# Six pools and their pads: where the tiles of a two-block float32 kernel begin in SBUF

## The chip, the cores and the metric

The kernel runs on one core of one Trainium2 chip. The metric is the device time of one launch in microseconds (us), the median of several runs. The profile is of one execution on the same core.

## What is computed

The reference is two transformer blocks on a sequence of 256 tokens of width 1024, each block two layers deep, all in float32:

```python
def first_block(x, c, ...):                       # 2 layers
    mod = silu(c) @ w_ada[l] + b_ada[l]
    h = rms_norm(x, g_norm1[l]) * (1 + sc1) + sh1
    u = h @ w_in[l] + b_in[l]
    y_mla = causal_softmax_attention(q, k, v_mla)
    y_sb = stick_breaking_attention(q_sb, k_sb, v_sb)
    merged = sigmoid(gate_mla) * (y_mla @ w_branch_mla[l]) + sigmoid(gate_sb) * (y_sb @ w_branch_sb[l])
    x = x + gt1 * (merged @ w_out[l])
    up = causal_depthwise_conv(h2 @ w_up[l], w_conv[l], b_conv[l])
    x = x + gt2 * ((silu(a) * v_ff) @ w_down[l])  # d_ff 2816

def second_block(x, c, ctx, ...):                 # 2 layers, latent and context tokens
    p = modulate(rmsnorm(x), sh1, sc1) @ w_in[l]
    x = x + gt1 * latent_mixer(p, ctx_kv, ...)    # global and window attention, short conv, gates
    x = x + gt2 * expert_choice_ffn(h2, ...)      # 16 experts, 32 tokens each, hidden 1024
```

The weights are read from HBM once; the page counts 739 MB.

## The kernel before

Activations stand feature-major: a tile `[128, 8, 256]` holds 1024 features in eight slices of 128 partitions and 256 tokens, so a slice is 1024 bytes of each partition. Tiles are taken by tag in `Kernel.t` (line 154): each tag has a fixed number of slots in the pool `sb`, and the tags lie one after another in the order in which they are first used.

Most products are made of float32r parts. A weight block comes by DMA into a `w` tile; `split` (line 216) has ScalarE cast it into `wh` and VectorE subtract the cast into `wl`. The activations are split likewise: `hh` and `hl` hold the normalized input of a layer, `pt` the merged branches of the second block, `k1` and `k8` the outputs of heads, branches and the feed-forward. `mm3` (line 229) then issues three matmuls for each slice of 128 features:

```python
for k in range(len(w)):
    (wh, wl), (xh, xl) = w[k], x[k]
    ops += [(wh, xh), (wh, xl), (wl, xh)]
for i, (a, b) in enumerate(ops):
    self.last_mm = self.nc.tensor.matmul(ps, a, b, ...)   # line 235
```

The first operand is the stationary one: 128 columns, 512 bytes of each partition, loaded by a LDWEIGHTS of its own. The second is the moving one: 256 columns, 1024 bytes. So in the order of TensorE's queue the moving operand goes `hh`, `hl`, `hh` slice by slice while the stationary ones go `wh`, `wh`, `wl`. In `first_layer`, `ffn` (`lower`, line 828, with the products of the feed-forward in two `k1` tiles), `mixer` and `out_proj` all large products run so. `tokens` (line 716) and part of `kv` have it the other way round, with `hh` or `hl` stationary and `wh` or `wl` moving. The products of the experts (`product`, line 1239, and line 1291) are plain float32 with 32 stationary columns, and their moving operands are the weights as they come by DMA, in `w`, `k8`, `k4`, `hh`, `hl`, `wh` and `wl` slots. Plain float32 matmuls are two instructions each on TensorE.

Where the tags lie follows from the widths of the tiles ahead of them. In the program before, `k1` and `k8` begin 384 bytes past a multiple of 1024, `w` 960, and `hh`, `hl`, `k2`, `wh`, `wl`, `k4` and `pt` all 320. Slices of a stationary operand are 512 bytes apart and slices of a moving one 1024. So the moving operand begins 0 or 512 bytes (mod 1024) from the stationary one where it is `hh`, `hl` or `pt`, and 64 or 576 where it is `k1` or `k8`. In the rows of a profile buffer numbers are left out: `k` stands for `k1`, `k2`, `k4` and `k8` together.

Of the kernel before, what the change touches and what calls it, by code (L numbers as in the profile page):

```python
# [9 lines left out]
F32 = mybir.dt.float32  # L10
# [7 lines left out]
P = 128  # L18
# [20 lines left out]
NH = 3  # L39
HALVES = {"k4": ("k4", "k4"), "whl": ("wh", "wl")}  # L40
BUFS = {"k4": N4, "wh": NH, "wl": 3}

CONST_WIDTHS = [
    [("ident", P), ("slot", 1), ("freq", 1), ("eps", 1), ("halfpi", 1), ("one", 1), ("sign", 1), ("ones", P), ("mask_m", P)],
# [53 lines left out]
class Stats:  # L98
    def __init__(self, kernel, x, bank=None, proj=None):
        self.kernel, self.x, self.ps, self.bank, self.proj = kernel, x, None, bank or kernel.ad, proj  # L100
# [22 lines left out]
class Kernel:  # L123
    def __init__(self, tc, ctx, io, out, consts):
        self.tc, self.nc, self.io, self.out = tc, tc.nc, io, out
        self.n = 0
        self.one = ctx.enter_context(tc.tile_pool(name="one", bufs=1))
        self.sb = ctx.enter_context(tc.tile_pool(name="sb", bufs=1))
        self.ps = ctx.enter_context(tc.tile_pool(name="ps", bufs=1, space=PSUM))
        self.cst = self.one.tile([P, NCONST], F32, name="cst")  # L130
        self.nc.sync.dma_start(self.cst[:, :NFIRST], consts[:, :NFIRST])
        self.consts = consts
        self.rt = self.one.tile([P, 2, S], F32, name="rope")
        self.fill = []
        self.wsel = 0
        self.table, self.head, self.users, self.before = None, None, [], []
        self.hook, self.last_mm = None, None
        self.ada_tags, self.ada_tag = [], "w"
# [14 lines left out]

    def t(self, shape, tag, bufs, dt=F32):
        self.n += 1
        return self.sb.tile(list(shape), dt, name=f"{tag}_{self.n}", tag=tag, bufs=bufs)

    def k8(self, shape, dt=F32):
        return self.t(shape, "k8", N8, dt)
# [43 lines left out]
    def wload(self, src, k0, nk, c0, nc_, tag="w"):  # L203
        t = self.wtile([P, nk, nc_], tag)
        self.nc.sync.dma_start(t, src[k0 * P:(k0 + nk) * P, c0:c0 + nc_].rearrange("(k p) n -> p k n", p=P))
        return t
# [19 lines left out]
    def wsplit1(self, src, shape):  # L226
        return self.wsplit(shape, [(src, lambda t: t)])
# [73 lines left out]
    def to_fm(self, src_dram, dst):  # L301
        nc = self.nc
        tm = self.k8([P, 2, D])
        nc.sync.dma_start(tm, src_dram.rearrange("(t p) d -> p t d", p=P))
        for t in range(2):
            for g in range(2):
                ps = self.mm((P, 4, P))
                for i in range(4):
                    k = 4 * g + i
                    nc.tensor.transpose(ps[:, i], tm[:, t, k * P:(k + 1) * P], self.c("ident"))  # L310
                nc.vector.tensor_copy(dst[:, 4 * g:4 * g + 4, t * P:(t + 1) * P], ps)
# [874 lines left out]
    def expert_loads(self, l, early, ring):  # L1186
# [13 lines left out]
        def more(n):  # L1200
            late = []
            for _ in range(min(n, len(todo))):
# [3 lines left out]
                if tag in HALVES:  # L1206
                    parts = [self.t([P, nk // 2, width], i, BUFS[i]) for i in HALVES[tag]]
                else:
# [267 lines left out]
```

## Time and profile before

| | |
|---|---|
| median of 3 runs | 2857.3 us (2854.14 to 2861.59) |
| profiled execution | 2864.09 us, of which the span is 2862.3 us |
| PE busy | 2663.3 us (93%) in 18816 matmul instructions |
| of these on line 235 | 10572 |
| DVE, ACT, POOL busy | 1406.6, 1022.9, 122.8 us |
| DMA | 742.61 MB, mean 259 GB/s, up to 409 GB/s in slices of 71.6 us |
| mean granted TensorE clock | 0.972 |

PE rows give matmuls; their ends are modelled and overlap, so the time that one takes in a stream is read from the distance of two starts, or from a stretch divided by its number of matmuls, and not from the duration in the row. PEld rows give the loads of stationary operands, which overlap the matmul ahead of them. A MATMUL row is named after its output, its moving and its stationary operand (`dd<-hh,wh`).

### The profile page before, as it was taken

What the parts mean: (1) busy time and instruction counts of PE and PEld (TensorE: products, weight loads), DVE (VectorE), ACT (ScalarE), POOL (GpSimd) and SP (SyncE); (2) the same over time, 40 slices, a digit from 0 to 9 for tenths busy, and PEclk for the clock granted to TensorE, in tenths of its full rate; (3) what the DMA queues carried; (4) which work ended last, traced back from release to release, by engine and by line L of the source; (5) the groups of instructions that cost most, each with busy time, mean ns of one, the idle gap of its engine ahead of it and who ended that gap; (6) DMA issues with size and microseconds to landing.
All of it is one profiled execution on the core that took longest, in us unless ns stands there. A gap on an engine that the chain in (4) does not pass through costs nothing.

```text
span 2862.3 us, 45431 instructions
## 1 busy us (share of the span) xinstructions
PE 2663.3 (93%) x18816; PEld 1847.5 (65%) x18816; DVE 1406.6 (49%) x2791; ACT 1022.9 (36%) x1906; POOL 122.8 (4%) x139
## 2 busy tenths in 40 slices
PE   7998999999999999899999999999899998877776
PEld 4898998888998689756994333333566994212122
DVE  5989977756777755776552011010577552000001
ACT  3564555554555644445453000001455442000000
POOL 0100001000000000120011000000021001000000
PEclk7999999999999999979999999999999999999998
DMA  8697855687555579412755999999712866999999
GB/s 291 226 325 273 319 175 164 199 267 230 171 178 192 162 247 268 140 39 82 199 162 219 367 401 401 409 402 389 248 62 71 262 213 261 409 409 408 409 409 318
DMA packets 397692, 742.61 MB, mean 259 GB/s; under 512 B 16214, under 2 KB 270126, under 8 KB 397486
## 3 DMA queue, kind: packets, MB, share of 16 engines
q1 hardware_dynamic: 396398, 738.66, 72.6%
q8 instruction: 148, 2.42, 0.3%
q10 hardware_dynamic: 1088, 1.05, 0.1%
q14 instruction: 58, 0.48, 0.0%
HBM read 738.61 MB, written 1.05 MB: 258 GB/s over the span
## 4 chain that ended last, share of the span: by engine, by line
PE 39%; DMA 13%; DVE 2%; POOL 1%; ACT 1%; SPq 0%; issue 0%; DVEq 0%; POOLq 0%; ACTq 0%
PE dd L235 12%; PE acc L1239 12%; PE mm L1239 5%; DMA w<-in_w_e_down_dram 3%; DMA w<-in_w_e_up_dram 2%; DMA k<-in_w_e_down_dram 2%; PE acc L931 2%; DMA k<-in_w_e_gate_dram 2%; DMA k<-in_w_e_up_dram 2%; DMA w<-in_w_e_gate_dram 2%; PE mm L960 1%; PE mm L954 1%; PE acc L1291 1%; PE dd L1272 1%; POOL k L746 1%; PE mm L1169 1%
## 5 line engine op out<-in xcount | busy, mean ns | idle before, releaser
L235 PE MATMUL dd<-hh,wh 128*128 128x256 f32 x2384 | 692.2, 292 | 17.6 <-ACT hh L259 13.9
L218 DVE TENSOR_TENSOR wl<-w,wh 128x1024 fp32r<-128x1024 f32 (+1 forms) x534 | 555.3, 1043 | 284.8 <-ACT wh L217 283.3
L235 PE MATMUL dd<-hh,wl 128*128 128x256 f32 x2384 | 684.8, 288 | 5.6 <-DVE wl L218 5.6
L235 PE MATMUL dd<-hl,wh 128*128 128x256 f32 x2384 | 684.0, 287 | 0.5 <-DVE hl L471 0.3
L217 ACT CAST wh<-w 128x1024 fp32r<-128x1024 f32 (+1 forms) x534 | 477.2, 899 | 563.5 <-PE dd L235 426.7
L235 PEld LDWEIGHTS dd<-hh,wh 128*128 128x128 f32 x2384 | 460.9, 194 | 43.6 <-ACT hh L259 15.6
L235 PEld LDWEIGHTS dd<-hh,wl 128*128 128x128 f32 x2384 | 461.3, 194 | 12.4 <-DVE wl L218 6.7
L235 PEld LDWEIGHTS dd<-hl,wh 128*128 128x128 f32 x2384 | 462.0, 194 | 10.0 <-issue 7.2
L1239 PE MATMUL acc<-w,pt 128*32 128x512 f32 x624 | 226.1, 605 | 34.5 <-DMA w<-in_w_e_up_dram 18.1
L1261 DVE TENSOR_TENSOR wh<-wh,acc 128x512 f32<-128x512 f32 x20 | 13.8, 688 | 460.3 <-PE acc L1239 460.3
L1239 PE MATMUL acc<-k,pt 128*32 128x512 f32 x692 | 227.7, 602 | 9.7 <-DMA k<-in_w_e_up_dram 5.8
L235 PE MATMUL dd<-k,wh 128*128 128x256 f32 x896 | 164.6, 283 | 1.8 <-DVE k L619 1.0
L746 POOL TENSOR_TENSOR k<-k,rope 32x256 f32<-32x256 f32 (+1 forms) x96 | 86.5, 901 | 1838.6 <-DVE k L890 1339.1
L1239 PE MATMUL acc<-w,k 128*32 128x512 f32 x480 | 160.6, 607 | 0.6 <-ACT pt L1139 0.6
L1239 PE MATMUL acc<-w,wl 128*32 128x512 f32 x396 | 140.1, 602 | 17.1 <-DMA w<-in_w_e_down_dram 17.1
L1239 PE MATMUL acc<-k,wl 128*32 128x512 f32 x432 | 147.0, 600 | 6.0 <-DMA k<-in_w_e_down_dram 6.0
L235 PEld LDWEIGHTS dd<-k,wh 128*128 128x128 f32 x896 | 137.5, 188 | 5.9 <-DVE k L619 1.6
L1239 PEld LDWEIGHTS acc<-w,pt 128*32 128x32 f32 x624 | 46.4, 110 | 138.3 <-issue 72.5
L1239 PE MATMUL acc<-k,k 128*32 128x512 f32 x376 | 133.2, 604 | 0.0
L235 PE MATMUL dd<-k,wl 128*128 128x256 f32 x448 | 125.2, 280 | 1.7 <-DVE wl L218 1.6
L1273 DVE SCALAR_TENSOR_TENSOR x_res<-dd,mod,x_res 128x256 f32<-128x256 f32 x64 | 28.9, 483 | 178.1 <-PE dd L1272 178.1
L1239 PEld LDWEIGHTS acc<-k,pt 128*32 128x32 f32 x692 | 46.0, 109 | 99.7 <-issue 65.3
(351 smaller groups left out, 4475.1 us busy)
## 6 DMA issues: line engine op xcount, KB each, us to landing
w<-in_w_in_dram SPq DMA_DIRECT2D x104, 1024.0 KB
w<-in_w_ada_dram SPq DMA_DIRECT2D x63, 1024.0 KB
w<-in_w_e_gate_dram SPq DMA_DIRECT2D x54, 1024.0 KB
w<-in_w_e_up_dram SPq DMA_DIRECT2D x54, 1024.0 KB
w<-in_w_e_down_dram SPq DMA_DIRECT2D x48, 1024.0 KB
w<-in_w_up_dram SPq DMA_DIRECT2D x44, 1024.0 KB
k<-in_w_e_gate_dram SPq DMA_DIRECT2D x43, 1024.0 KB
k<-in_w_e_down_dram SPq DMA_DIRECT2D x43, 1024.0 KB
```

The lines of the kernel that those rows point to most:

```text
L217: self.nc.scalar.copy(h, src)
L218: self.nc.vector.tensor_tensor(l, src, h.bitcast(F32), op=OP.subtract)
L235: self.last_mm = self.nc.tensor.matmul(ps, a, b, start=first and i == 0, stop=last and i == len(ops) - 1, skip_group_check=group)
L746: nc.gpsimd.tensor_tensor(u[dst], q[src], sin[src], op=OP.mult)
L931: nc.tensor.matmul(ps[:, :n], q[a, mt, qb * P:(qb + 1) * P], kk[a, br, lo:512], start=True, stop=not mask, skip_group_check=True)
L954: nc.tensor.transpose(pp[:, i], e[:, i * P:(i + 1) * P], self.c("ident"))
L960: nc.tensor.matmul(po[64 * f:64 * f + 64], vv[:, kt, P * br + 64 * f:P * br + 64 * f + 64], pt[:, f, i], start=i == 0, stop=i == len(kts) ...
L1169: nc.tensor.matmul(ps, th[:, t, a], b, start=t == 0, stop=False)
L1239: nc.tensor.matmul(accs[s][n][32 * e:32 * e + 32], lhs(s, 2 * kp + k, e), tiles[e][k][:, 512 * n:512 * n + 512], start=kp == 0 and k == 0, ...
L1272: nc.tensor.matmul(ps, y[:, k * P:(k + 1) * P], maps[s][:, gi], start=True, stop=True)
L1273: nc.vector.scalar_tensor_tensor(x[:, k], ps, gate[:, k:k + 1], x[:, k], op0=OP.mult, op1=OP.add)
L1291: nc.tensor.matmul(ps[32 * e:32 * e + 32], down(s, k, e), tiles[e][k], start=k == 0, stop=k == KT - 1, skip_group_check=True)
```

## The change

Twelve of the tags leave the pool `sb` for six pools of their own, which lie ahead of it in this order; some pools begin with a gap tile that no instruction touches. `PADS` counts float32 columns, so the gaps are 64, 32, 32, 128 and 32 bytes. The pool `one` gets a tile of 128 bytes that is not used either. Slots per tag, shapes, instructions and their order stay as they are.

```diff
+PLACES = [("wh", "wl", "w", "k2", "k4", "rx", "rr"), ("hh",), ("hl",), ("k1",), ("k8",), ("pt",)]
+PADS = [0, 16, 8, 8, 32, 8]
+PAD = 32
...
         self.one = ctx.enter_context(tc.tile_pool(name="one", bufs=1))
+        self.pools = {}
+        for n, tags in enumerate(PLACES):
+            pool = ctx.enter_context(tc.tile_pool(name=f"hot{n}", bufs=1))
+            self.pools |= {tag: pool for tag in tags}
+            if PADS[n]:
+                pool.tile([P, PADS[n]], F32, name=f"gap{n}")
         self.sb = ctx.enter_context(tc.tile_pool(name="sb", bufs=1))
...
         self.rt = self.one.tile([P, 2, S], F32, name="rope")
+        self.pad = self.one.tile([P, PAD], F32, name="pad")
...
     def t(self, shape, tag, bufs, dt=F32):
         self.n += 1
-        return self.sb.tile(list(shape), dt, name=f"{tag}_{self.n}", tag=tag, bufs=bufs)
+        return self.pools.get(tag, self.sb).tile(list(shape), dt, name=f"{tag}_{self.n}", tag=tag, bufs=bufs)
```

In the program before, the pool `one` ends at byte 20352 of each partition. With 128 bytes more, the first new pool begins at 20480, a multiple of 1024. All slots of these pools are multiples of 1024 bytes wide, so by the widths alone the tags come to lie, past a multiple of 1024:

| tag | before | changed | from `wh` and `wl`, before | changed |
|---|---|---|---|---|
| `wh`, `wl`, `w`, `k2`, `k4` | 320 (`w` 960) | 0 | | |
| `hh` | 320 | 64 | 0 | 64 |
| `hl` | 320 | 96 | 0 | 96 |
| `k1` | 384 | 128 | 64 | 128 |
| `k8` | 384 | 256 | 64 | 256 |
| `pt` | 320 | 288 | 0 | 288 |

Half of the stationary slices lie 512 bytes further, before and after.

## Rows read from the trace of the kernel before

**Rows 1.** The page's slices: busy tenths of engines, granted clock, DMA.

```profile
PE   7998999999999999899999999999899998877776
PEclk7999999999999999979999999999999999999998
GB/s 291 226 325 273 319 175 164 199 267 230 171 178 192 162 247 268 140 39 82 199 162 219 367 401 401 409 402 389 248 62 71 262 213 261 409 409 408 409 409 318
```

**Rows 2.** Stretches of the whole kernel: time, busy time and instructions by engine, clock, DMA.

```profile
core 0: us, PE busy (x) PEld busy (x) DVE busy (x) ACT busy (x) POOL busy (x), PEclk, DMA share, GB/s
210.00:290.00 80.00, 70.79 (x537) 67.09 (x536) 75.99 (x121) 39.78 (x64) 0.00 (x0) 0.94 0.79 278
290.00:465.00 175.00, 173.88 (x1407) 166.09 (x1405) 147.26 (x217) 93.38 (x141) 0.00 (x0) 1.00 0.66 228
725.00:910.00 185.00, 182.59 (x1508) 179.48 (x1508) 134.91 (x223) 102.00 (x162) 0.00 (x0) 0.99 0.48 162
1080.00:1480.00 400.00, 384.03 (x2785) 323.28 (x2783) 263.12 (x537) 194.01 (x368) 36.31 (x45) 0.96 0.49 148
1560.00:2050.00 490.00, 484.40 (x3468) 179.69 (x3468) 53.46 (x110) 48.81 (x94) 0.00 (x0) 0.99 1.00 385
2450.00:2862.00 412.00, 317.57 (x1476) 87.83 (x1476) 21.32 (x42) 12.10 (x22) 0.00 (x0) 0.97 1.01 394
```

**Rows 3.** Line 235 by operands: count, duration in ns (min/median/max), first and last start, shape.

```profile
L235 PEld LDWEIGHTS dd<-hh,wh x2384: 186/192/338, 44.2 to 2333.3; 128*128 128x128 f32 x199
L235 PEld LDWEIGHTS dd<-hl,wh x2384: 186/192/338, 44.4 to 2333.4; 128*128 128x128 f32 x199
L235 PEld LDWEIGHTS dd<-hh,wl x2384: 186/192/333, 48.9 to 2333.5; 128*128 128x128 f32 x199
L235 PEld LDWEIGHTS dd<-pt,wh x416: 186/192/329, 1154.6 to 2369.3; 128*128 128x128 f32 x139
L235 PEld LDWEIGHTS dd<-pt,wl x208: 186/192/329, 1154.9 to 2369.4; 128*128 128x128 f32 x104
L235 PEld LDWEIGHTS dd<-k,wh x896: 186/188/193, 78.4 to 2336.2; 128*128 128x128 f32 x180
L235 PEld LDWEIGHTS dd<-k,wl x448: 186/188/192, 80.6 to 2336.3; 128*128 128x128 f32 x150
L235 PEld LDWEIGHTS acc<-k,wh x528: 186/187/193, 278.0 to 891.0; 128*128 128x128 f32 x176
L235 PEld LDWEIGHTS acc<-k,wl x264: 187/188/190, 278.2 to 891.1; 128*128 128x128 f32 x132
L235 PEld LDWEIGHTS mm<-k,wh x176: 187/187/192, 280.1 to 891.7; 128*128 128x128 f32 x176
```

**Rows 4.** The chain of waits, 1345.2 to 1375.6 us: start, us, what.

```profile
1345.16 30.55 PE dd L235 x253
```

**Rows 5.** PE in order of time: start, us, what; the moving operand changes twice.

```profile
1375.90 0.40 PE L235 MATMUL dd<-k,wh 128*128 128x256 f32 x2
...
1376.26 0.40 PE L235 MATMUL dd<-k,wh 128*128 128x256 f32 x2
...
1378.38 0.40 PE L235 MATMUL dd<-k,wh 128*128 128x256 f32 x2
...
1378.74 0.29 PE L235 MATMUL dd<-hh,wh 128*128 128x256 f32 x1
...
1379.46 0.28 PE L235 MATMUL dd<-hh,wh 128*128 128x256 f32 x1
```

**Rows 6.** PE in order of time, another stretch with `k` moving.

```profile
200.11 0.39 PE L235 MATMUL dd<-k,wh 128*128 128x256 f32 x2
...
201.81 0.28 PE L235 MATMUL dd<-k,wh 128*128 128x256 f32 x1
```

**Rows 7.** Two lines of plain float32 matmuls: count, duration in ns, shape.

```profile
L110 PE MATMUL ad<-k,cst x160: 377/379/795, 10.8 to 2371.1; 128*128 128x256 f32 x160
L1272 PE MATMUL dd<-k,k x192: 379/379/483, 1659.2 to 2857.1; 128*128 128x256 f32 x192
```

## The prediction, made before the changed kernel was run

> **What bounds the kernel now.** I read the slices of the page first, then the same by stretches, and only then single instructions. The slices show TensorE at nine tenths nearly throughout, with two long parts in which DMA runs at 401 to 409 GB/s [rows 1]. The stretches separate the two. From 290 to 465, 725 to 910 and 1080 to 1480 us TensorE is busy 174 of 175, 183 of 185 and 384 of 400 us, while DMA moves 148 to 228 GB/s; from 1560 to 2050 and from 2450 on, the experts, DMA has a share of 1.00 [rows 2]. So the first kind is bound by how fast TensorE gets through its queue, the second by HBM. [...] Most of the first kind is line 235; by the code the experts have none of it.
>
> What one matmul of line 235 costs is the distance of two starts. With `hh` and `hl` moving, 253 matmuls take 30.55 us [rows 4]. Taking off the last one's modelled end (0.28 us, as in rows 5) leaves 30.27 us for 252 distances, 120.1 ns each. With `k` moving, 18 matmuls start between 1376.26 and 1378.38 us, 117.8 ns each [rows 5]; the shape is the same. The weight loads say it too: the median of 2384 loads is 192 ns with `hh` or `hl` moving, 192 with `pt`, and 187 or 188 with `k` [rows 3]. Five groups of the one kind agree, and five of the other (some `k2` are among the `k`): the tile that moves decides. One thing that separates these tiles is where the program puts them: `hh`, `hl` and `pt` begin 0 or 512 bytes from the stationary operand (mod 1024), `k1` and `k8` 64 or 576. And `k` can be faster still: in one stretch 15 matmuls start within 1.70 us, 113.3 ns each [rows 6]. The shortest load is 186 ns in nearly all groups [rows 3], so 113.3 is close to the best that the trace shows.
>
> **The change part by part.** It adds no instruction and no wait. Each tag keeps its number of slots, so what waits for a slot is as before; the pad tiles are never touched. What moves is the place of twelve tags, and I price that by who reads them.
>
> *`hh`, `hl` and `pt` moving on line 235.* 3 x 2384 + 416 + 208 = 7776 matmuls [rows 3]. `hh`, two thirds of the first 7152, goes to 64, the distance that `k` has now. `hl` goes to 96 and `pt` to 288, which no row shows. Bounds for these are 113.3 and 120.1 ns [rows 6, 4]; I take 117.8, as 96 lies next to 64. The sum is 7776 x (120.1 - 117.8) = 17.9 us. If `hl` and `pt` stay at 120.1, 3008 x 2.3 = 6.9 us of it are lost.
>
> *`k1` and `k8` moving on line 235.* 896 + 448 + 528 + 264 + 176 = 2312 matmuls are shown [rows 3]. They leave 64 for 128 and 256. Bounds are again 113.3 and 120.1, so between 2312 x 4.5 = 10.4 us less and 2312 x 2.3 = 5.3 us more. I take nothing, since the rows give no reason to leave 117.8.
>
> *The rest of line 235,* 10572 - 7776 - 2312 = 484 matmuls, mostly with weights moving past `hh` and `hl`: at 2.3 ns either way 1.1 us; I take nothing.
>
> *Plain float32.* Line 110 moves a `k1` tile and line 1272 a `k4` tile, which lie in the two different places, and both have a median of 379 ns [rows 7]: no difference by place, so nothing. For the experts' line 1239 the four stationary operands of a step lie 128 bytes apart, so all distances occur there before and after; besides, DMA sets the time.
>
> *The other engines and DMA.* ScalarE and VectorE read and write the moved tiles. Where TensorE sets the time they have slack: VectorE is busy 147 of 175 and 263 of 400 us [rows 2]. If their accesses became slower by a tenth, that would still lie beside the matmuls there. Only from 210 to 290 us is VectorE the fuller one, 76 of 80 us against 71 [rows 2]; a faster TensorE may bring nothing in that stretch, 537 x 2.3 = 1.2 us. DMA writes into `w`, `k8` and `hh` slots, at 960, 384 and 320, and still moves 401 to 409 GB/s [rows 1]; of the new places only those of `hl` and `pt` are no multiples of 64. I take nothing, with both signs possible.
>
> What a faster TensorE triggers: weight slots come free earlier and loads start earlier. In its stretches DMA has room for that (0.48 to 0.66 of its share [rows 2]). The experts' stretches then begin earlier and last as long, so the gain is kept to the end.
>
> The sum is 17.9 less 1.2, about 17 us. The profiled execution took 2864.1 us, its span 2862.3 and 1.8 around it; it would take 2847. The median of the runs is 6.8 us below that execution, and I forecast from the median: 2857.3 - 17 = 2840 us, with 2833 to 2848 if single tags turn out otherwise.
>
> **The rivals.**
>
> *Further than the row.* If the new distances all let matmuls run as in the stretch with 113.3 ns, 7776 x 6.8 + 2312 x 4.5 = 63 us go, 2794 us. For it: that rate exists, with the same shapes and tiles. Against it: the same `k` tiles run at 117.8 elsewhere, so 64 alone doesn't bring it, and `hh` gets just that 64.
>
> *The place itself counts, not the distance.* All stationary tiles lie at 320 now, so the rows cannot tell a distance of 64 from a moving operand at 384, a multiple of 128. If a multiple of 128 is what makes `k` fast, `hh` at 64, `hl` at 96 and `pt` at 288 stay slow, as 320 is, `k1` at 128 and `k8` at 256 stay fast, and the time stays at 2857 us (2853 to 2861). Nothing in the rows speaks against it. The same time follows if two reads of TensorE don't touch each other at all and the two kinds differ by something else that goes with the tile, such as who wrote it last.
>
> [...]
>
> *The alternation costs more than the distance brings.* Now `hh` and `hl` lie alike; after the change `mm3` moves 64, 96, 64, so the place changes at two of three matmuls. Rows 5 hold two such changes: from 1375.90 to 1379.46 us there are 24 distances with `k` and 6 with `hh`. At their steady rates they would take 24 x 117.8 + 6 x 120.1 = 3548 ns; they take 3560, so a change costs some 6 ns, and with rows rounded to 10 ns anything from 0 to 11. Two changes in each of 2384 triples are 4768; at 6 ns that is 28.6 us, and 28.6 - 17 = 12 us slower, 2869 us. It turns the sign from 17 / 4768 = 3.6 ns a change on. Against it: the step is 32 bytes and not 64, and a change back and forth may settle into a rhythm of its own.
>
> **How the numbers follow.** I give 0.44 to the forecast (2833 to 2848), 0.12 to the further gain (2794 and what lies between), 0.22 to the place itself or no effect, 0.16 to the alternation, and 0.06 to a loss that I have not priced, such as slower accesses to `hl` and `pt`. A measurement of this kernel tells about 0.3%, 8.6 us, from no change. Faster than that is the forecast and the further gain, 0.56; the same is the third case and a little of the others, 0.24; slower is 0.20. The likeliest case gives 2840. The range takes in the middle of the further gain and of the alternation: 2797 to 2866.
>
> **What would show it.** In the changed kernel's rows for line 235, loads with `hh` moving should have a median of 188 instead of 192 ns, and a stretch of `hh` and `hl` matmuls some 118 ns each. If loads with `hh` stay at 192 while `k` stays at 188, the place itself counts. If `hh` at 64 and `hl` at 96 show distances that differ within a triple and together exceed 360 ns, the alternation costs. Loads with `k` moving tell what 128 and 256 are worth: 186 would be better than now, 192 worse. The experts' stretches should be as long as before. The forecast is wrong if distance has no steady effect, or if TensorE's gain is eaten by VectorE, which would show as waits for `wl` on line 235.

## The result and the profile after

The changed kernel takes 2828.3 us (median of 4 runs, 2826.6 to 2837.9) against 2855.7 us of the kernel before in the same comparison (2851.5 to 2861.6): a ratio of 0.990, 95% interval 0.9884 to 0.9916. The gain is 27 us where 17 were forecast. Of line 245 (235 before) comes about a third of it; the rest goes with the rate of DMA, which the forecast had priced at nothing.

The profiled execution before (2864.1 us) began at a lower granted clock, 0.7 in its first slice [rows 1]. So the kernel before was profiled once more, as the first experiment, and the comparison below goes by that second trace, **before_again**. Two lines of its page, the span and the queue that carries nearly all loads (packets, MB, share of the time of 16 engines):

```profile
span 2856.9 us, 45431 instructions
q1 hardware_dynamic: 396398, 738.66, 73.0%
```

The same lines of the changed kernel, with the slices of clock and DMA that answer to [rows 1]:

```profile
span 2827.2 us, 45431 instructions
PEclk9999999999999999989999999999999999999999
GB/s 310 242 314 290 309 176 169 186 277 240 163 193 191 151 257 266 138 43 80 204 164 221 366 401 404 420 388 409 248 60 75 250 235 222 420 420 420 421 420 344
q1 hardware_dynamic: 396398, 738.66, 71.5%
```

What to see: the same packets and bytes, in less time of the engines. 0.730 x 16 x 2856.9 us / 396398 is 84.2 ns of an engine for a packet, 0.715 x 16 x 2827.2 / 396398 is 81.6. The last long stretch runs at 420 GB/s where [rows 1] show 409 (before_again has 409 too, see the first experiment).

Line 245 by operands in the changed kernel (count, ns as min/median/max, first and last start), which answers to [rows 3]:

```profile
L245 PEld LDWEIGHTS dd<-hh,wh x2384: 186/188/338, 37.2 to 2311.9; 128*128 128x128 f32 x199
L245 PEld LDWEIGHTS dd<-hl,wh x2384: 186/188/338, 37.4 to 2312.0; 128*128 128x128 f32 x199
L245 PEld LDWEIGHTS dd<-k,wh x896: 186/192/330, 70.2 to 2314.9; 128*128 128x128 f32 x180
L245 PEld LDWEIGHTS acc<-k,wh x528: 186/188/193, 269.6 to 877.1; 128*128 128x128 f32 x176
...
L245 PEld LDWEIGHTS dd<-pt,wh x416: 186/188/192, 1140.4 to 2347.7; 128*128 128x128 f32 x139
```

Loads with `hh`, `hl` and `pt` moving went from 192 to 188 ns. The `k` with output `dd` is `k8`, now 256 bytes from the stationary operand: 188 became 192. The `k` with output `acc` is `k1`, at 128: 187 became 188.

The same groups also date the gain, because each row has its first and last start. In before_again:

```profile
L235 PEld LDWEIGHTS dd<-hh,wh x2384: 186/192/337, 40.5 to 2328.2; 128*128 128x128 f32 x199
L235 PEld LDWEIGHTS acc<-k,wh x528: 186/187/193, 273.4 to 886.1; 128*128 128x128 f32 x176
L235 PEld LDWEIGHTS dd<-pt,wh x416: 186/192/331, 1149.8 to 2364.2; 128*128 128x128 f32 x139
```

The first load with `hh` starts 40.5 - 37.2 = 3.3 us earlier, the first with `k1` 3.8, the last with `k1` 9.0, the first with `pt` 9.4, the last with `hh` 16.3, the last with `pt` 16.5, and the end comes 29.7 earlier. So 13.2 us appear after the last matmul of line 245, in the stretch that the forecast said would be as long as before. The two long blocks of line 245 in the chain of waits (start, us, what), in before_again

```profile
1340.33 128.27 PE dd L235 x1072
...
2204.05 127.65 PE dd L235 x1067
```

and in the changed kernel

```profile
1329.34 127.45 PE dd L245 x1072
...
2188.54 126.85 PE dd L245 x1067
```

give 0.8 us each. From the end of the first to the start of the second, which holds the first experts' stage, it is 735.4 us before (2204.05 - 1340.33 - 128.27) and 731.8 after, 3.6 less. So the start and the last stretch give 3.3 + 13.2 = 16.5 us, and the other 13.2 are spread over what lies between. Some 9 of these are line 245 (worked out further down); what the rest hangs on was not followed.

The first experts' stage gave back so little because loads do not set its pace, and did not before the change either. In before_again, from 1520 to 1990 us, TensorE's waits show one for a load (waits of TensorE: us in total, times, longest):

```profile
PE acc L1291 <- DMA w<-in_w_e_down_dram: 1.2, 1, 1.2
```

Its products (line 1239, now 1249) take 458.2 us from the first start to the last in before_again and 457.1 in the changed kernel. The DMA share of 1.00 in [rows 2] says that loads were always under way there, not that TensorE waited for them. In the last stretch it does wait. From 2365 us on, the longest of its waits for loads in before_again is

```profile
PE acc L1239 <- DMA w<-in_w_e_up_dram: 19.4, 19, 2.8
```

and with the waits for other loads it comes to some 93 us.

The start is where the rate of loads shows first: the first 40 us, in before_again

```profile
0.00:40.00 40.00, 22.87 (x181) 12.91 (x181) 16.72 (x56) 9.05 (x19) 0.20 (x4) 0.92 0.98 308
```

and in the changed kernel

```profile
0.00:40.00 40.00, 24.04 (x185) 14.13 (x185) 20.23 (x66) 12.09 (x24) 0.20 (x4) 0.95 0.98 330
```

have the same share of DMA, 0.98, and 308 against 330 GB/s.

Of two kernels further down, apart64 and apart32, the profile was taken in a disturbed execution (a TensorE clock of 0.66 and 0.57), and none of their rows are used.

### The profile page after: what moved, and what is told of

The parts are those of the page before. It is cut to its first block, busy times and chain, and to the rows that moved or that the text cites. A ratio compares the mean times of both kernels' runs of the same rounds, so it can differ in the third digit from the quotient of the medians.

```text
span 2827.2 us, 45431 instructions
## 1 busy us (share of the span) xinstructions
PE 2637.7 (93%) x18816; PEld 1835.7 (65%) x18816; DVE 1406.4 (50%) x2791; ACT 1023.5 (36%) x1906; POOL 123.2 (4%) x139
## 3 DMA queue, kind: packets, MB, share of 16 engines
q1 hardware_dynamic: 396398, 738.66, 71.5%
## 4 chain that ended last, share of the span: by engine, by line
PE 39%; DMA 12%; DVE 3%; POOL 1%; SPq 1%; ACT 1%; issue 0%; DVEq 0%; POOLq 0%; ACTq 0%
PE dd L245 12%; PE acc L1249 12%; PE mm L1249 5%; DMA w<-in_w_e_up_dram 2%; DMA k<-in_w_e_down_dram 2%; PE acc L941 2%; DMA w<-in_w_e_down_dram 2%; DMA k<-in_w_e_gate_dram 2%; DMA k<-in_w_e_up_dram 2%; DMA w<-in_w_e_gate_dram 2%; PE mm L970 1%; PE mm L964 1%; PE acc L1301 1%; PE dd L1282 1%; POOL k L756 1%; SPq L1208 1%
## 5 line engine op out<-in xcount | busy, mean ns | idle before, releaser
L245 PE MATMUL dd<-hh,wh 128*128 128x256 f32 x2384 | 684.4, 288 | 17.6 <-ACT hh L269 13.9
L245 PE MATMUL dd<-hh,wl 128*128 128x256 f32 x2384 | 677.9, 285 | 5.6 <-DVE wl L228 5.6
L245 PEld LDWEIGHTS dd<-hh,wh 128*128 128x128 f32 x2384 | 454.2, 191 | 42.9 <-ACT hh L269 15.6
L245 PEld LDWEIGHTS dd<-hh,wl 128*128 128x128 f32 x2384 | 451.7, 190 | 12.5 <-DVE wl L228 6.9
L245 PEld LDWEIGHTS dd<-hl,wh 128*128 128x128 f32 x2384 | 452.6, 190 | 10.2 <-issue 7.2
L941 PE MATMUL acc<-k,k 64*128 64x512 f32 (+1 forms) x192 | 94.5, 606 | 14.8 <-ACT k L269 9.5
```

The lines of the kernel that those rows point to most:

```text
L245: self.last_mm = self.nc.tensor.matmul(ps, a, b, start=first and i == 0, stop=last and i == len(ops) - 1, skip_group_check=group)
L941: nc.tensor.matmul(ps[:, :n], q[a, mt, qb * P:(qb + 1) * P], kk[a, br, lo:512], start=True, stop=not mask, skip_group_check=True)
```

## The experiments

Places are given past a multiple of 1024 bytes, as in the table ahead. All edits are to the three constants of the change. The times, each beside runs of the kernel before on the same chip (its medians 2858.7 to 2860.1 us, 2855.7 for the changed kernel):

| kernel | us, median | ratio, 95% interval | moving from `wh`, `wl` | loads' destinations | last stretch, GB/s |
|---|---|---|---|---|---|
| changed | 2828.3 | 0.9884 to 0.9916 | `hh` 64, `hl` 96, `k1` 128, `k8` 256, `pt` 288 | `w`, `k8` at multiples of 256, `hh`, `hl` off | 420 |
| shift64 | 2850.9 | 0.9960 to 0.9985 | as changed | `w`, `k8` 64 past a multiple of 256 | 409 |
| shift128 | 2849.9 | 0.9960 to 0.9980 | as changed | `w`, `k8` 128 past one | 409 |
| shift256 | 2829.9 | 0.9878 to 0.9905 | as changed | `w`, `k8` at multiples of 256, `hh`, `hl` off | 420 |
| flat | 2840.2 | 0.9919 to 0.9956 | all 0 | all at 0 | 420 |
| flat_w64 | 2845.6 | 0.9930 to 0.9957 | all 0 | `w` 64 past, others at 0 | 420 |
| k_at_64 | 2832.0 | 0.9881 to 0.9912 | as changed, but `k1`, `k8` 64 | `w`, `k4` at 0, `k8`, `hh`, `hl` off | 419 |
| apart64, and again | 2826.0, 2812.9 | 0.9851 to 0.9900, 0.9826 to 0.9869 | all 64 | all at 0 | 420 |
| apart128 | 2836.8 | 0.9897 to 0.9936 | all 128 | all at 0 | 420 |
| apart32 | 2826.3 | 0.9861 to 0.9902 | all 32 | all at 0 | no rows used |
| apart64_shift64 | 2840.5 | 0.9909 to 0.9936 | all 64 | all 64 past | 409 |

A distance of 64 means 64 or 576, since half of the stationary slices lie 512 bytes further; so it is with all of them.

**The kernel before once more.** No edit.

> The kernel before, unchanged, profiled again beside the other kernels of this group. In the changed kernel the experts' saturated slices moved 420 GB/s and in the profile of before 409 GB/s. If the place of the DMA's destinations does that, this run shows 401 to 409 GB/s there again, and the median of the weight loads with hh moving is 192 ns, with k moving 187 to 188. If the two profiles only differ by the run they come from, this one shows some 420 GB/s and a span some 10 to 15 us under 2862.

Its lines stand above. The medians of the loads of line 235 are those of [rows 3] within 1 ns, and queue 1 takes 73.0% against 71.5. DMA ends at 409 GB/s again; its totals from 2450 to 2760 us (packets, MB, rate) are

```profile
DMA packets 33115, 126.84 MB, mean 409 GB/s; under 512 B 2178, under 2 KB 2178, under 8 KB 33103
```

The difference in DMA belongs to the kernel and not to the chip or the execution: flat, further down, ran on the same chip and has 420.

**The same distances, other places.** Three kernels move all twelve tags together, and with them what lies behind, the rest of `sb`.

```diff
-PAD = 32
+PAD = 48
```

(64 bytes further), `PAD = 64` (128) and `PAD = 96` (256).

> The changed kernel with 64 bytes more ahead of the six pools: all distances between moving and stationary operands stay, all places move by 64 bytes. If the distance counts, line 235's loads keep the changed kernel's medians (188 ns with hh, hl and pt moving, 192 with k8) and so do the stretches of its matmuls. If the place itself counts, with multiples of 128 the good ones, hh now at 128 is fast but k1 at 192 and k8 at 320 are slow, and pt at 352 too. If the DMA's gain hangs on destinations at multiples of 256, w, k4 and k8 lose it: 401 to 409 GB/s in the experts, some 13 us more there and some 8 us more at the start, about 2848 us. If DMA does not depend on the place, the time stays at 2828 us.

> The changed kernel moved by 128 bytes: distances as in the changed kernel, DMA destinations w and k4 at 128, k8 at 384. Loads on line 235 keep the changed kernel's medians. If the DMA needs destinations at multiples of 256 (or more), the experts' slices show 409 GB/s as with 64 bytes, and the time is some 2850 us; if multiples of 128 are enough, 420 GB/s and 2828 us.

> All twelve tags 256 bytes further on than in the changed kernel: every distance between moving and stationary operands is the same, and w, k2, k4, k1 and k8 still begin at multiples of 256 (w at 256, k8 at 512). Theory 1, that loads are fast where their destination begins at a multiple of 256: 420 GB/s in the last stretch, queue 1 at 71.2 to 71.8 %, about 2828 us (2822 to 2835), as the changed kernel. Theory 2, that the changed kernel's w is fast because it begins at a multiple of 512 or of 1024: 409 GB/s, queue 1 at 73 %, about 2850 us, as with shifts of 64 and 128. The weight loads of TensorE are the same under both: 188 ns with hh, 192 with k8.

Loads of line 245 in shift64:

```profile
L245 PEld LDWEIGHTS dd<-hh,wh x2384: 185/188/338, 43.0 to 2321.2; 128*128 128x128 f32 x199
...
L245 PEld LDWEIGHTS dd<-k,wh x896: 186/192/193, 77.2 to 2324.2; 128*128 128x128 f32 x180
```

188 with `hh` at 128 and 192 with `k8` at 320, as with `hh` at 64 and `k8` at 256: what counts for TensorE is the distance, not the place. shift128 and shift256 have the same medians.

For DMA it is the place. The same totals of DMA from 2450 to 2760 us, in shift64

```profile
DMA packets 33103, 126.83 MB, mean 409 GB/s; under 512 B 2169, under 2 KB 2169, under 8 KB 33091
```

in shift128

```profile
DMA packets 33113, 126.84 MB, mean 409 GB/s; under 512 B 2177, under 2 KB 2177, under 8 KB 33101
```

in shift256

```profile
DMA packets 34000, 130.29 MB, mean 420 GB/s; under 512 B 2223, under 2 KB 2223, under 8 KB 33987
```

and in the changed kernel

```profile
DMA packets 33992, 130.25 MB, mean 420 GB/s; under 512 B 2223, under 2 KB 2223, under 8 KB 33979
```

Shifts of 64 and 128 bytes lose the rate and some 21 us of time, one of 256 loses neither. Only the place modulo 256 of the loads' destinations goes with it. The places are worked out from the widths of the tiles, since no run prints an address; that pads of 128 and 384 bytes have the rate and pads of 192 and 256 lose it agrees with them. This also gives the worth of the distances by themselves: shift64 and shift128 are 0.3% faster than the kernel before, 8 us (4 to 11 by the interval of shift64).

**DMA by itself.** All pads at zero, so that all twelve tags lie at 0 and all distances are 0.

```diff
-PADS = [0, 16, 8, 8, 32, 8]
+PADS = [0, 0, 0, 0, 0, 0]
```

> The changed kernel without gaps between its six pools: hh, hl, k1, k8, pt, wh and wl all begin at multiples of 1024, so every distance on line 235 is 0 or 512. If the distance counts, all loads have a median of 192 ns and a matmul takes 120 ns; against the changed kernel 7776 matmuls lose some 1.8 ns each and 968 with k1 some 1.5, about 15 us: 2843 us. If the place itself counts, multiples of 128 being good, all loads have 188 and the time is at or under 2828 us. DMA destinations are all at multiples of 1024: 420 GB/s in the experts if their place counts for DMA.

```profile
L245 PEld LDWEIGHTS dd<-hh,wh x2384: 186/192/338, 37.4 to 2325.4; 128*128 128x128 f32 x199
...
L245 PEld LDWEIGHTS dd<-k,wh x896: 186/192/331, 70.7 to 2328.4; 128*128 128x128 f32 x180
```

All loads are at 192, those with `k` too; TensorE is slower than in the kernel before, and still the time is 18 us less. That is the DMA gain with what `k` lost taken off.

**Distances, with DMA aligned.** All moving operands go into one pool at 0, `wh` and `wl` into a second one at 448; the distances are 64 or 576 for every pair, and `hh` and `hl` no longer differ.

```diff
-PLACES = [("wh", "wl", "w", "k2", "k4", "rx", "rr"), ("hh",), ("hl",), ("k1",), ("k8",), ("pt",)]
-PADS = [0, 16, 8, 8, 32, 8]
+PLACES = [("w", "k2", "k4", "rx", "rr", "hh", "hl", "k1", "k8", "pt"), ("wh", "wl")]
+PADS = [0, 112]
```

apart64_again is the same kernel. apart32 has `PADS = [0, 120]` (distances of 32 or 544), apart128 `PADS = [0, 96]` (128 or 640).

> hh, hl, k1, k8, pt, w and k4 all at multiples of 1024 in one pool, wh and wl in a second one 448 bytes past a multiple, so every moving operand of line 235 begins 64 or 576 bytes from its stationary one. If the distance counts and 64 is good for each tile, all loads have medians of 187 or 188 ns and a matmul takes 117.8 ns; against the changed kernel k8's 1344 matmuls gain some 2.3 ns and the alternation of 64 and 96 is gone (7152 matmuls, some 0.5 ns): 6 to 7 us less, 2821 us. If the place itself counts, it is as the kernel without gaps.

> The kernel with wh and wl 448 bytes past a multiple of 1024 and all other moved tags at multiples of 1024, once more for a profile at the full clock. If the distance counts: loads with hh, hl, pt, k1 and k8 moving all have medians of 187 or 188 ns, a matmul takes 117.8 ns, the time is 2821 us. If the place counts, loads are as in the kernel without gaps, 192 ns.

> As before, but wh and wl 480 bytes past a multiple, so that every distance is 32 or 544. In the changed kernel pt at 288 had the shortest times (a matmul about 117 ns) and k8 at 256 the longest, as at 0. If the distance counts with a period of 256, 32 is as good as 288: some 117 ns a matmul instead of 117.8, and 10000 matmuls give 8 us: 2813 us. If the period is not 256 and 288 is good by itself, 32 is anything between 0 and 64, 117.8 to 120 ns: 2821 to 2840 us.

> As before, with wh and wl 384 bytes past a multiple: every distance is 128 or 640, that of k1 in the changed kernel (medians 188 ns there, matmuls between 113 and 122 ns, 118.4 in the mean). If the distance counts alone, all line 235 runs as k1 there: 2824 us. If k1's spread comes from the changing mixture of tiles and not from 128, a single rate shows, 113 to 120 ns: 2785 to 2840 us.

apart64_again takes 2812.9 us (2809.5 to 2823.1), 0.985 of the kernel before, and beats the changed kernel. The same kernel took 2826.0 us as apart64 (2820.0 to 2829.3), hardly less than the changed kernel; 2821 was expected, which lies between the two. All loads of line 245 have a median of 187 or 188 ns:

```profile
L245 PEld LDWEIGHTS dd<-hh,wh x2384: 186/188/337, 43.2 to 2305.7; 128*128 128x128 f32 x199
...
L245 PEld LDWEIGHTS dd<-k,wh x896: 186/188/192, 77.2 to 2308.5; 128*128 128x128 f32 x180
```

The load's median hides finer steps; apart128 has 188 as well and is slower. They show in the long blocks of the chain. Flat:

```profile
1336.20 128.83 PE dd L245 x1072
```

apart128:

```profile
1331.93 127.40 PE dd L245 x1072
```

apart64_again:

```profile
1329.93 126.46 PE dd L245 x1072
...
2187.92 121.13 PE dd L245 x1067
```

Taking off the last modelled end (0.28 us) and dividing by 1071 distances: 120.0 ns at a distance of 0, 118.7 at 128, 117.8 at 64. In the second block of apart64_again it is 120.85 / 1066 = 113.4 ns, the rate of [rows 6], held through a whole block. apart128 and flat have no such block. One block at 113.4 ns is some 5 us shorter than at 117.8, so how many blocks have it may be what separates apart64 from apart64_again; without usable rows of apart64 that is not shown.

apart128 took 2836.8 us (2828.3 to 2841.2) where 2824 was expected if it ran as `k1` did in the changed kernel. A single rate shows, as in the second case of the expectation. It is 0.3 ns a matmul above the mean of the changed kernel (118.7 against 118.4, table below), some 3 us; the rest of the difference is not explained. apart32 (2826.3 us) lies in the range of the second case of its expectation and not at the 2813 of the first, so 32 does not bring what a period of 256 would; without rows nothing more can be said of it.

**The distance without the DMA gain.** apart64, moved by 64 bytes as a whole.

```diff
-PAD = 32
+PAD = 48
```

> The kernel with all moving operands 64 or 576 bytes from wh and wl, moved by 64 bytes as a whole: the distances stay, and the destinations of the loads (w, k2, k4, k8, hh, hl) begin 64 past a multiple of 256. Theory 1, that the two gains are separate and add: TensorE keeps its gain (loads of 187 to 188 ns, as before the shift), the DMA gain goes (409 GB/s, queue 1 at 73 %), and the time is 2813 + 20 = 2833 us (2828 to 2840), 25 us under the kernel before. Theory 2, that the distance brings time only where DMA is fast too: about 2850 us or more.

```profile
1330.91 121.69 PE dd L245 x1072
...
2191.58 125.86 PE dd L245 x1067
```

TensorE keeps its rates (113.4 ns in the first block, 125.58 / 1066 = 117.8 in the second; which block has the faster rate has changed), and DMA falls back:

```profile
DMA packets 33105, 126.82 MB, mean 409 GB/s; under 512 B 2174, under 2 KB 2174, under 8 KB 33093
```

2840.5 us (2834.8 to 2847.0) lies just past the upper edge of what the first theory gave (2828 to 2840) and 10 us under the second's 2850. The two gains are separate: from the kernel before, the distance alone gives 20 us (this one); flat gives 18, in which line 245 has lost some 6 (the means further down, 10572 x 0.55 ns), so DMA alone is worth some 24. Both give 46 us in apart64_again, where they nearly add, and 33 in apart64.

**Who must lie at a multiple of 256?** flat_w64 puts `w` alone off by 64; k_at_64 puts `k1` and `k8` at 64, which also gives `k` the distance that it had before.

```diff
 # flat_w64
+PLACES = [("wh", "wl", "k2", "k4", "rx", "rr"), ("hh",), ("hl",), ("k1",), ("k8",), ("pt",), ("w",)]
+PADS = [0, 0, 0, 0, 0, 0, 16]
 # k_at_64
+PLACES = [("wh", "wl", "w", "k2", "k4", "rx", "rr"), ("hh", "k1", "k8"), ("hl",), ("pt",)]
+PADS = [0, 16, 8, 48]
```

> The kernel with all pads at zero, with w alone in a last pool 64 bytes past a multiple of 256; k2, k4, k8, hh, hl stay at multiples of 1024. Theory 1, that each load pays for its own destination: nearly all bytes of the experts go to w, so 409 to 411 GB/s in the last stretch, queue 1 at 72.5 to 73 %, and 2852 to 2858 us, nearly all of the 18 us that separate the flat kernel from the one before. Theory 2, that the loss comes only where many different tags begin off 256: 420 GB/s and 2840 us.

> The changed kernel with k1 and k8 at 64 instead of 128 and 256; hh, hl, pt and w as they were. TensorE: if 64 is worth for k what it was worth before the change, weight loads with k8 moving go from 192 back to 188 ns and 1.5 to 2 ns go from each of some 2000 distances, 3 to 4 us; if what slowed k8 was something else than its distance, they stay at 192. DMA: k8 takes about a third of the 4096-byte packets and 8 % of the 1024-byte ones. If each load pays for its own destination alone, that gives back 3 to 6 us, so about 2828 us in all (2822 to 2834); if any unaligned tag slows all loads, 409 GB/s and 2844 us or more.

For flat_w64 the first theory fell: with `w` off, the last stretch keeps its rate.

```profile
DMA packets 34005, 130.27 MB, mean 420 GB/s; under 512 B 2230, under 2 KB 2230, under 8 KB 33993
```

In k_at_64, with `k8` off (and `hh`, `hl`), it loses 1 GB/s, so one tag off doesn't slow all loads to 409. The rows below it are the loads into `w` and `k4` in the same stretch of k_at_64. By the code only `k4` tiles are loaded in halves of 512 KB there, and `k4` lies at 0 as `w` does:

```profile
DMA packets 33875, 129.80 MB, mean 419 GB/s; under 512 B 2216, under 2 KB 2216, under 8 KB 33863
...
w<-in_w_e_up_dram SPq DMA_DIRECT2D x18, 1024.0 KB
w<-in_w_e_gate_dram SPq DMA_DIRECT2D x16, 1024.0 KB
...
w<-in_w_e_down_dram SPq DMA_DIRECT2D x12, 1024.0 KB
k<-in_w_e_gate_dram SPq DMA_DIRECT2D x12, 512.0 KB
k<-in_w_e_up_dram SPq DMA_DIRECT2D x12, 512.0 KB
k<-in_w_e_down_dram SPq DMA_DIRECT2D x8, 512.0 KB
```

46 loads of 1.049 MB and 32 of 0.524 are 65 of 130 MB, so half of the bytes go to multiples of 256, and that is nearly enough for the full rate. In flat_w64 `w` takes 47 loads, 38% of the bytes, and having these off costs no rate at all. My assumption that "nearly all bytes of the experts go to `w`" was wrong by these rows.

The rate of the last stretch doesn't fall in step with the bytes that lie off a multiple of 256: it is 409 GB/s with all of them off (shift64, shift128), 419 with half (k_at_64), and 420 with 38% (flat_w64) and with none (flat).

What flat_w64 does lose is in the first 40 us, where weights are loaded into `w` at 314 GB/s

```profile
0.00:40.00 40.00, 22.68 (x182) 12.58 (x183) 17.50 (x59) 9.81 (x20) 0.20 (x4) 0.89 0.96 314
```

instead of 328 in flat:

```profile
0.00:40.00 40.00, 22.77 (x185) 13.30 (x185) 19.89 (x65) 12.09 (x24) 0.20 (x4) 0.95 0.97 328
```

The granted clock differs in these two as well, 0.89 and 0.95, but it is not what sets the rate of the loads: apart64_again, with `w` at 0, has 327 GB/s at 0.75.

```profile
0.00:40.00 40.00, 26.71 (x180) 13.12 (x180) 14.04 (x47) 7.29 (x15) 0.20 (x4) 0.75 0.97 327
```

The time of flat_w64 is 1 to 5 us above that of flat (by the ratios and by the medians).

For TensorE, k_at_64 answers what was asked: loads with `k8` moving are back at 188.

```profile
L245 PEld LDWEIGHTS dd<-k,wh x896: 186/188/337, 70.5 to 2312.4; 128*128 128x128 f32 x180
```

So it was the distance of 256 that slowed `k8`. In the profile the last `hh` starts at 2309.5 us, 2.4 before that of the changed kernel. The time doesn't show it (2832.0 against 2828.3 us, with overlapping intervals); part of it is lost again in the last stretch, 129.8 MB at 419 GB/s instead of 420 being 0.7 us, and the rest can't be told from the scatter of the runs.

## Why the prediction was right and where it was wrong

All distances of line 245, taken together, are in the next table: the mean in ns from one start to the next over pairs of neighbours of 256 columns that lie under 150 ns apart (9760 to 9830 pairs in each trace).

| kernel | `hh`, `hl` | `pt` | `k8` | `k1` | all |
|---|---|---|---|---|---|
| before | 119.8 | 119.4 | 117.5 | 117.9 | 119.3 |
| changed | 118.3 | 117.1 | 119.7 | 118.4 | 118.4 |
| flat | 119.8 | 119.6 | 119.9 | 120.0 | 119.8 |
| k_at_64 | 118.3 | 117.0 | 117.8 | 117.8 | 118.1 |
| apart128 | 118.7 | 118.6 | 118.7 | 118.7 | 118.7 |
| apart64_again | 117.1 | 117.7 | 116.1 | 117.5 | 116.9 |

The means of apart64_again take in its blocks at 113.4 ns.

- **The distance decides: right.** The sign of the change, its tags and the mark that was named (192 to 188 with `hh`) came as said, and the shifts separate distance from place. Had the two kinds differed only by something that goes with the tile, as the second rival allowed, kernels with the same tiles at other places would be alike on TensorE; flat at 120.0 ns and apart64_again at 117.8 in the same block are not.
- **`hh`, `hl`, `pt`: 17.9 us was too much.** 7152 x (119.8 - 118.3) + 624 x 2.3 is 12.2 us. The step that failed is the size of the difference: 120.1 was read in one stretch where the mean is 119.8, and 117.8 was taken from `k`, which moves alone, while `hh` and `hl` take turns.
- **`k`: nothing was the wrong middle.** `k8` lost 1344 x 2.2 = 3.0 us, `k1` 968 x 0.5 = 0.5, near the bound of 5.3 that the prediction had. The rows gave no price for 256; the runs say that it is nearly as bad as 0, and that 128 lies between.
- **Line 245 in all** gained 12.2 - 3.5, some 9 us, half of the forecast; shift64, which has the distances and not the DMA, measured 8.
- **DMA: "I take nothing" is the term that failed.** It is worth some 19 of the 27 us (27 less 8; 21 by the shifts). The argument was that DMA moved 401 to 409 GB/s with its destinations at 960, 384 and 320 [rows 1]. That is a high rate, but nothing in the rows said what the same loads do elsewhere, so it bounded no gain; the bound above zero was missing. With it fell "the experts' stretches as long as before": the last one is 13.2 us shorter.
- **"The second by HBM" was read from the share of DMA alone.** In the first experts' stage TensorE waited for a load once, for 1.2 us, so DMA did not bound it. In the last stretch DMA did, but the rate rose with nothing changed but places in SBUF, so HBM was not the limit at 409 GB/s.
- **The total was partly luck.** 2828 lies in the whole range (2797 to 2866), which is wide, but not in the 2833 to 2848 that the likeliest case was given. It falls between that case and the further gain, which had 0.12, and for another cause: TensorE gave about half of its 17 us, and DMA, at nothing in the sum, gave some 19. The two errors have opposite signs.
- **The alternation was priced far too high.** In the changed kernel, line 245 in order of time (start, us):

```profile
1329.73 0.28 PE L245 MATMUL dd<-hh,wl 128*128 128x256 f32 x1
1329.85 0.28 PE L245 MATMUL dd<-hh,wh 128*128 128x256 f32 x1
1329.97 0.28 PE L245 MATMUL dd<-hl,wh 128*128 128x256 f32 x1
1330.09 0.28 PE L245 MATMUL dd<-hh,wl 128*128 128x256 f32 x1
...
1359.55 0.28 PE L245 MATMUL dd<-hh,wl 128*128 128x256 f32 x1
1359.67 0.40 PE L245 MATMUL dd<-k,wh 128*128 128x256 f32 x2
...
1362.54 0.28 PE L245 MATMUL dd<-hh,wh 128*128 128x256 f32 x1
```

  From 1329.73 to 1359.55 lie 84 triples of `hh`, `hh`, `hl`, 355 ns each or 118.3 a matmul, under the 360 that the prediction gave as the mark. At the same distance of 64 and without taking turns a matmul takes 117.8 (apart64_again). The 0.5 ns is 1.5 a triple, 0.8 ns for each of two changes where 6 were taken; it may also be the price of 96 against 64, since no run has `hl` alone at 96. After the switch, 24 matmuls with `k8` take 2.87 us, 119.6 each, where [rows 5] have 117.8.
- **The further gain exists, but not here.** 113.4 ns was held through whole blocks in apart64_again and apart64_shift64, never in the changed kernel.

**What stays open.** Why a matmul takes TensorE 2 ns more at a distance of 0 or 256 bytes than at 64 (120.0 and 119.7 against 117.8, each with 512 more for half of the slices), and one more at 128 (118.7): the runs show that it does and not how. What starts the 113.4 ns rate: the same kernel, only shifted, has it in another block. And how destinations off a multiple of 256 bytes bring DMA from 420 to 409 GB/s: the runs show the rates and no cause.

## What to carry to other kernels

Put the destinations of large loads at multiples of 256 bytes (420 GB/s here, 409 with all of them off), and let moving and stationary operands of a dense stream of matmuls like these begin 64 or 576 bytes apart where both are free to choose: here the two together took 33 to 46 us from 2859 (two sets of runs of one kernel), of which the distance alone gave 20. Check what else a pad moves: a shift by 64 or 128 bytes that leaves every distance as it was cost 21 us through DMA. A DMA share of 1.00 doesn't say that anyone waits (in the first experts' stage of before_again, at 0.99, TensorE waited for a load once, for 1.2 us); read the waits. And a resource at its usual rate is no proof that the rate can't rise (409 GB/s became 420); a term without a row that bounds it from above deserves a bound, not a zero.

## What the runs showed of the hardware that was not expected

- In the last stretch, 2450 to 2760 us, loads of 4096-byte rows ran at 420 GB/s with destinations at multiples of 256 bytes (flat) and at 409 with all of them off (shift64); with half of the bytes aligned they still had 419 (k_at_64), and with 62% all of the 420 (flat_w64).
- The distance of two matmuls of 128x128 by 256 columns went with where the moving operand begins from the stationary one: 120.0 ns at 0 (flat), 119.7 at 256 (`k8` of the changed kernel), 118.7 at 128 (apart128), 117.8 at 64 (first block of apart64_again), each a mean with the same distance and 512 bytes more.
- At 64 (and 576) the stream had two rates, 117.8 and 113.4 ns, and kept one through a block of over a thousand matmuls (apart64_again, apart64_shift64); at 128 (apart128) and 0 (flat) the long blocks had only one, 118.7 and 120.0.
